# Next weights split ahead of the value loops, two tiles for the value copies, and TensorE in program order with its transposes two units late

## The chip, the cores and the metric

One core of a Trainium2 chip runs the kernel. The metric is the device time of one execution in microseconds (us). PE is the matrix engine (TensorE), DVE the vector engine, ACT the scalar engine, POOL GpSimd, SP the engine whose queue issues the DMAs here.

## The reference

The kernel computes one block of a streaming encoder over 1024 tokens of width 1024, in float32: three token mixers in parallel (multi-head latent attention, MLA; forgetting attention, FoX; a state-space mixer), a gated merge, and a gated MLP. What the change touches is the end of MLA's projections, the projection `u = hn @ w_in` for FoX and for the gate `z`, and FoX's normalisation and decay sums:

```python
hn = rms_norm(x, norm_mix_g[l])
u = hn @ w_in[l]
u_mla, u_fox, u_ssm, u_gate = jnp.split(u, split_at, axis=-1)
# fox_branch
q, k, v, f_raw = jnp.split(u, [FOX_WIDTH, 2 * FOX_WIDTH, 3 * FOX_WIDTH], axis=-1)
q = rms_norm(q.reshape(Bsz, S, FOX_HEADS, FOX_HEAD_DIM), q_gain)
k = rms_norm(k.reshape(Bsz, S, FOX_HEADS, FOX_HEAD_DIM), k_gain)
v = v.reshape(Bsz, S, FOX_HEADS, FOX_HEAD_DIM)
log_f = jax.nn.log_sigmoid(f_raw.astype(jnp.float32) + b_f.astype(jnp.float32))
F = jnp.transpose(jnp.cumsum(log_f, axis=1), (0, 2, 1))
# ssm_branch
z, xBC, dt_raw = jnp.split(u, [SSM_INNER, SSM_INNER + SSM_XBC], axis=-1)
```

## The kernel before, in words

Every float32 operand of a product is split into a high and a low part (`split`, lines 138 to 143: ACT writes the high part, line 142, DVE the rest, line 143), and `mm3` (line 167) sums three products for each of 8 blocks of the inner dimension: 24 matmuls a unit. Tokens come in 8 tiles of 128.

From about 95 to 426 us these things run:

- The MLA loop (`for t in range(NT)`, lines 450 to 507): for each token tile the products q and kv, a normalisation (`rq`), a rotation on POOL (`rope`, lines 443 to 448, of which the last instruction, line 448, writes `qn`), four groups of transposes (tiles `tp`, line 500), copies of those out of PSUM (`sh` by ACT, line 503; `sl` by DVE, line 504), and stores to DRAM (`q_h`, `q_l`, `k_h`, `k_l`, line 507). `sh` and `sl` have two buffers each; a store must land before its tile is written again.
- The value loop (lines 510 to 519): FoX's value projection, two halves of 256 columns, each of 8 tiles, each 24 matmuls (`fxv`). The products are copied and split into one tile, `fv`, with one buffer, and stored to `fv_d`. The weights are `v`, the second half's are loaded between the halves.
- 32 units of 24 matmuls with 512 columns (`fx`, lines 640 to 684): 8 of the first half of z (z0), 8 of FoX q, 8 of FoX k, 8 of the second half of z (z1); I number them 0 to 31. `load512` loads and splits their weights: four raw pieces of 512 KB each, split into `w5h` and `w5l`, each of which has two tags in turn. Raw tiles (`raw`, two buffers) come from the pool `fill`. A z unit ends in a tanh (`th`, line 654), a product (`zt`, line 656) and a store. A FoX unit ends in a square on ACT (`fsq`, line 661), a sum (`fss`, line 663), 12 small DVE operations of an inverse root (`rsqrt`, lines 148 to 159, on `rs_i`, `rs_t`, `rs_v`, `fr`) behind one on `fv` (line 665), the normalised tile (`fqn`, line 669), a group of four transposes on PE (line 673), copies (`fsh` on ACT, `fsl` on DVE) and stores.
- `gate_sums` (lines 560 to 612): cumulative sums and transposes (lines 562 to 609) for the decays.
- `down_sums` (lines 627 to 638), at two of every five units up to the 27th: two loads of 512 KB (`ws`), four sums on POOL (lines 633 to 636), two stores (`wsum_d`), work for the MLP at the end.

Behind these come the weights `wr`, `wh`, `wl` of the next projection (lines 741 to 745) and MLA's attention (lines 794 and 884).

No queue's order is written by hand here: a scheduler with a model of the engines lays the instructions of each engine in one fixed list, and each engine works through its list in order, waiting on semaphores. The loads and stores of this stretch are all issued by SP. Tiles are taken from pools that are stacked on the left or the right side of SBUF; a pool that opens where a closed one lay has its first writes wait for the last users of the old tiles. Before, `cos`, `sin`, the MLA loop's inputs (pool `chp`), its weights (`upp`) and its working tiles (`mp`) close together with the value loop's pool `fvp`, and `fill` and the units' pool `xp` open behind them.

## Time and profile before

| what | value |
|---|---|
| median of three runs | 2149.49 us (2144.91 to 2150.79) |
| the profiled execution's own time | 2144.91 us |
| its span in the trace | 2143.0 us |
| PE busy | 2042.3 us, 95% of the span |
| DVE, ACT, POOL busy | 1402.9, 936.0, 649.0 us |
| mean granted clock of PE | 0.982 |

The profiled execution was the fastest of the three; 1.9 us of it lie around the span. Rows of a timeline give the start in us, the duration in us, the engine, line and operation, what is written and read, and in brackets how long the engine stood idle before it and what ended that. A row of waits gives the engine, what it wanted to start, what it waited for, the sum, the count and the longest. The granted clock is 1.00 at 2.4 GHz and 0.50 at 1.2 GHz.

### The profile page before, as it was taken

To read this page: it belongs to the slowest core of one execution; us is meant where nothing else is said; L and a number is where in the kernel's file an instruction comes from. 1 tells how busy PE (TensorE), PEld (TensorE's weight loads), DVE (VectorE), ACT (ScalarE), POOL (GpSimd) and SP (SyncE) were. 2 spreads that over 40 slices of the span, in tenths; PEclk is the share of its full clock that TensorE was granted. 3 is DMA by queue.
4 is the path that set the end of the run, shared out by engine and by line. 5 is a ranking of instruction groups with operands and counts; after the bars stand their busy time and mean duration, and the time that the engine had idled before them with its cause. 6 is when DMAs were issued, how large, how long until landed. Compare 5 with 4: busy or idle time off the path is not lost.

```text
span 2143.0 us, 29100 instructions
## 1 busy us (share of the span) xinstructions
PE 2042.3 (95%) x10253; PEld 1689.7 (79%) x10253; DVE 1402.9 (65%) x2590; ACT 936.0 (44%) x1677; POOL 649.0 (30%) x620
## 2 busy tenths in 40 slices
PE   7999898999999999999999799999889999999999
PEld 6898677778888787787777688888668888887887
DVE  6687477346666566665888446557976677665665
ACT  5554222145555555554555213223444454545432
POOL 2453132212222222220000021002655544441855
PEclk9999999999999999999999899999899999999999
DMA  5167668654343544524342556441122222229765
GB/s 169 33 190 222 220 216 240 205 156 126 96 137 97 138 121 109 131 86 127 105 134 89 162 184 204 140 134 61 49 86 82 88 79 80 88 74 338 260 217 190
DMA packets 276649, 303.61 MB, mean 142 GB/s; under 512 B 19308, under 2 KB 209784, under 8 KB 276504
## 3 DMA queue, kind: packets, MB, share of 16 engines
q1 hardware_dynamic: 276504, 301.76, 46.0%
q8 instruction: 81, 1.33, 0.3%
q14 instruction: 64, 0.52, 0.1%
HBM read 209.03 MB, written 92.67 MB: 141 GB/s over the span
## 4 chain that ended last, share of the span: by engine, by line
PE 78%; DVE 7%; DMA 5%; POOL 3%; ACT 3%; issue 3%; SPq 0%; DVEq 0%; ACTq 0%; POOLq 0%
PE mm L794 16%; PE dn L1626 10%; PE ybr L167 8%; PE ua L1319 5%; PE fx L167 5%; PE uc L1319 5%; PE ud L1319 4%; PE wo L1364 4%; PE s L884 3%; PE tp L952 2%; PE ub L1319 2%; PE fxv L167 1%; DMA raw<-in_w_in_dram 1%; PE kv L167 1%; PE q L167 1%
## 5 line engine op out<-in xcount | busy, mean ns | idle before, releaser
L794 PE MATMUL mm<-hnh,wh 128*128 128x512 f32 x576 | 248.6, 432 | 0.0
L906 POOL TENSOR_SCALAR pm<-pm,rs 128x128 f32<-128x128 f32 (+7 forms) x128 | 110.2, 864 | 402.6 <-DVE rs L905 242.1
L794 PE MATMUL mm<-hnh,wl 128*128 128x512 f32 x576 | 226.9, 394 | 0.0
L794 PE MATMUL mm<-hnl,wh 128*128 128x512 f32 x576 | 226.1, 393 | 0.0
L1626 PE MATMUL dn<-dr,dr 128*128 128x512 f32 x592 | 182.1, 389 | 0.0
L899 ACT ACTIVATE pm<-s,nmx 128x128 f32<-128x128 f32 (+2 forms) x192 | 110.2, 579 | 97.6 <-DVE nmx L896 70.2
L958 DVE TENSOR_TENSOR ptl<-tp,pth 128x512 fp32r<-128x512 f32 (+1 forms) x160 | 100.2, 633 | 70.3 <-ACT pth L957 68.7
L889 DVE TENSOR_REDUCE nmx<-s 128x1 f32<-128x128 f32 (+2 forms) x192 | 105.5, 553 | 56.6 <-PE s L887 44.6
L884 PE MATMUL s<-qk,qk 96*128 96x384 f32 (+5 forms) x480 | 120.8, 356 | 13.0 <-ACT pm L899 11.4
L957 ACT ACTIVATE pth<-tp 128x512 fp32r<-128x512 f32 (+1 forms) x160 | 88.1, 554 | 99.5 <-PE tp L952 99.0
L1626 PEld LDWEIGHTS dn<-dr,dr 128*128 128x128 f32 x592 | 111.1, 188 | 22.9
L794 PEld LDWEIGHTS mm<-hnh,wl 128*128 128x128 f32 x576 | 108.4, 188 | 25.1
L794 PEld LDWEIGHTS mm<-hnl,wh 128*128 128x128 f32 x576 | 109.2, 190 | 17.1 <-issue 2.9
L794 PEld LDWEIGHTS mm<-hnh,wh 128*128 128x128 f32 x576 | 109.5, 190 | 16.6 <-issue 2.9
L1235 POOL TENSOR_TENSOR mg<-mg,gl 128x512 f32<-128x512 f32 x16 | 24.9, 1561 | 311.4 <-DVE gl L1232 311.3
L1626 PE MATMUL dn<-dr 128*128 128x512 f32 x296 | 115.2, 389 | 0.0
L167 PE MATMUL fx<-w5h,hnh 128*128 128x512 f32 x256 | 101.9, 402 | 7.9 <-ACT w5h L142 7.9
L143 DVE TENSOR_TENSOR dr<-dr,dr 128x1024 fp32r<-128x1024 f32 x52 | 75.3, 1449 | 49.9 <-ACT dr L142 41.8
L142 ACT ACTIVATE wh<-wr 128x1024 fp32r<-128x1024 f32 (+1 forms) x46 | 42.0, 913 | 147.6 <-PE ybr L167 69.6
L884 PEld LDWEIGHTS s<-qk,qk 96*128 96x128 f32 (+1 forms) x480 | 81.3, 192 | 26.4 <-ACT pm L899 16.2
L167 PE MATMUL ybr<-ah,wh 128*128 128x512 f32 x256 | 100.2, 396 | 1.6 <-ACT ah L142 1.6
L167 PE MATMUL fx<-w5h,hnl 128*128 128x512 f32 x256 | 101.4, 397 | 0.0
(457 smaller groups left out, 5855.7 us busy)
## 6 DMA issues: line engine op xcount, KB each, us to landing
dr<-act_d SPq DMA_DIRECT2D x99, 256.0 KB
wr<-in_ffn_w_up_dram SPq DMA_DIRECT2D x47, 512.0 KB
wr<-in_w_in_dram SPq DMA_DIRECT2D x36, 512.0 KB
g_d<-t SPq DMA_DIRECT2D x24, 512.0 KB
gl<-g_d SPq DMA_DIRECT2D x24, 512.0 KB
ws<-in_ffn_w_down_dram SPq DMA_DIRECT2D x22, 512.0 KB
wsum_d<-ws SPq DMA_DIRECT2D x22, 512.0 KB
act_d<-fa SPq DMA_DIRECT2D x22, 512.0 KB
```

What stands on the lines that cost most here:

```text
L143: return i, le.tensor_sub(l, src, f32(h))
L167: T.matmul(ps, a(k), b(k), start=(i == 0), stop=(i == n - 1))
L794: T.matmul(ps, a[:, k, :], b[half][:, k, :], start=(k == 0 and i == 0), stop=(k == NK - 1 and i == 2))
L884: T.matmul(ps[:, :w], q_[:, qs], k_[:, a:a + w], start=i_ == 0, stop=not last and i_ == len(o.passes) - 1)
L889: later(c + 0.1, lambda ps=ps, ci=ci, a=a, b=b: V.reduce_max(nmx[:, ci:ci + 1], ps[:, :b - a], axis=AX, negate=True))
L899: pss[ci][1][0] = later(c + 0.9 + 0.1 * ci, lambda ci=ci, a=a, b=b: A.activation(p_[:, a:b], pss[ci][0][:, :b - a], AF.Exp, bias=nb, accum ...
L906: G.tensor_scalar(p_[:, 0:n * P], p_[:, 0:n * P], rs[:, 3:4], 0.0, op0=ALU.mult, op1=ALU.add)
L957: later(c + 0.05, lambda th=th, pt=pt, off=off: A.activation(th[:, :off], pt[:, :off], AF.Copy))
L958: pl[0] = later(c + 0.6, lambda th=th, tl=tl, pt=pt, off=off: V.tensor_sub(tl[:, :off], pt[:, :off], f32(th[:, :off])))
L1319: T.matmul(ps, a, b, start=first and n == 0, stop=n == 11, skip_group_check=not first)
L1364: T.matmul(p, a, b, start=k == 0 and i == 0, stop=k == NK - 1 and i == 2)
L1626: T.matmul(ps[m], a[:, ts_], b[:, 512:], start=first_ and j == 0 and q == 0, stop=j == NFH - 1 and q == 2, skip_group_check=not first_)
```

## The change

- The pools `fvp` and `upp` go to a stack of their own on the right side (`pup`). The MLA loop's pools close right behind that loop, and `xp` opens in their place, ahead of the value loop.
- The second half's value weights (`v2`) and the first z weights (`w_z0`) are loaded and split ahead of both halves of the value loop in the program text; `v2` takes the tile tagged `w5l1`, and all four raw pieces of the z weights lie in the tile tagged `w5h1` (`w5r`), so that they need no raw buffers.
- The value products' copies of the second half take two tiles in turn (tags `fsh`, `fsl`) instead of the one `fv`.
- The units are built with PE's list in program order (`manual_schedule`), and the transposes of a FoX unit are called when two more units have been called (`waiting`, `turned`). `gate_sums` is a generator, of which one part is called after each unit from the first FoX unit on.

```diff
-    pmla = ExitStack()
+    pmla, pup = ExitStack(), ExitStack()
...
-        upp = pmla.enter_context(TP("upp", 1, side="right"))
+        upp = pup.enter_context(TP("upp", 1, side="right"))
...
-        fvp = pm.enter_context(TP("fvp", 1))
+        fvp = pup.enter_context(TP("fvp", 1, side="right"))
...
-        for c0 in (0, 256):
+    pmla.close()
+    px = ExitStack()
+    xp = px.enter_context(TP("xp", 2))
+    fpl = None
+    units = 0
+
+    def load512(c0):
+        n = units // NT % 2
+        h = xp.tile([P, NK, 512], F32R, name=uid("w5h"), tag=f"w5h{n}", bufs=1)
+        l = xp.tile([P, NK, 512], F32R, name=uid("w5l"), tag=f"w5l{n}", bufs=1)
+        if fpl is None:
+            raws_ = f32(xp.tile([P, NK, 512], F32R, name=uid("w5r"), tag="w5h1", bufs=1))
+        for k in range(0, NK, 2):
+            raw = raws_[:, k:k + 2, :] if fpl is None else fpl.tile([P, 2, 512], F32, name=uid("raw"), tag="wr")
+            SY.dma_start(raw, w_inv[:, k:k + 2, c0:c0 + 512])
+            split(h[:, k:k + 2, :], l[:, k:k + 2, :], raw)
+        return h, l
+
+    v2 = xp.tile([P, NK, 2, 256], F32R, name="v2", tag="w5l1", bufs=1)
+    for k in range(0, NK, 2):
+        raw = fvp.tile([P, 2, 256], F32, name=uid("raw"), tag="vr", bufs=2)
+        SY.dma_start(raw, w_inv[:, k:k + 2, C_FQ + 1280:C_FQ + 1536])
+        split(v2[:, k:k + 2, 0, :], v2[:, k:k + 2, 1, :], raw)
+    vcols.append((v2[:, :, 0, :], v2[:, :, 1, :]))
+    w_z0 = load512(C_Z)
+    for c0 in (0, 256):
+        vh, vl = vcols[c0 // 256]
+        for t in range(NT):
+            p = acc("fxv", "mv")[:, 0:256]
+            mm3(p, tok(hnh, t), tok(hnl, t), lambda k: vh[:, k, :], lambda k: vl[:, k, :], NK)
             if c0:
-                vcols.append(load_cols(fvp, "v", C_FQ + 1024 + c0, 256, 1))
-            vh, vl = vcols[-1]
-            for t in range(NT):
-                p = acc("fxv", "mv")[:, 0:256]
-                mm3(p, tok(hnh, t), tok(hnl, t), lambda k: vh[:, k, :], lambda k: vl[:, k, :], NK)
+                vt = xp.tile([P, 4, P], F32R, name=uid("fv"), tag=("fsh", "fsl")[t % 2], bufs=1)
+            else:
                 vt = fvp.tile([P, 4, P], F32R, name=uid("fv"), tag="fv", bufs=1)
-                split(vt[:, :, 0:64], vt[:, :, 64:128], p.rearrange("p (h d) -> p h d", d=64))
-                SY.dma_start(fv_d[t * P:(t + 1) * P, c0 // 64:c0 // 64 + 4, :], f32(vt))
-    pmla.close()
+            split(vt[:, :, 0:64], vt[:, :, 64:128], p.rearrange("p (h d) -> p h d", d=64))
+            SY.dma_start(fv_d[t * P:(t + 1) * P, c0 // 64:c0 // 64 + 4, :], f32(vt))
+    pup.close()
...
         T.matmul(pc[:, 64:128], ones, lf.rearrange("p t h -> p (t h)"), start=True, stop=True)
+        Ab = bcast(ssm_A_log[0], 16, "Ab", fp)
...
+        yield
...
+        trim = ft("trim", (P, P))
+        V.tensor_copy(trim, tri)
+        V.tensor_scalar_add(trim[0:64, :], trim[0:64, :], -1.0)
+        yield
...
         cum = ft("cum", (P, P))
         V.tensor_copy(cum, pd[:, 384:512])
+        yield
+        yield
         pt = tps([P, P])
         T.transpose(pt, cum, ident)
...
-    with ExitStack() as px:
-        xp = px.enter_context(TP("xp", 2))
...
+    with px:
...
-        units = 0
-        for which in (3, 0, 1, 4):
-            if which == 0:
-                gate_sums()
-            c0 = (C_FQ, C_FQ + 512, C_FQ + 1024, C_Z, C_Z + 512)[which]
-            wh, wl = load512(c0)
-            for t in range(NT):
-                if units % 5 in (1, 3) and units // 5 * 2 + units % 5 // 2 < NFH:
-                    down_sums(units // 5 * 2 + units % 5 // 2)
-                p = acc("fx", "mv" if units % 3 == 2 else "mm")
-                units += 1
-                mm3(p, tok(hnh, t), tok(hnl, t), lambda k: wh[:, k, :], lambda k: wl[:, k, :], NK)
...
-                    pt = tps()
-                    for j in range(4):
-                        T.transpose(pt[:, j, :], qn[:, 2 * j:2 * j + 2, :].rearrange("p h d -> p (h d)"), ident)
...
+        gs = gate_sums()
+        waiting = []
+
+        def turned(which, t, qn):
+            pt = tps()
+            for j in range(4):
+                T.transpose(pt[:, j, :], qn[:, 2 * j:2 * j + 2, :].rearrange("p h d -> p (h d)"), ident)
+            col = (fq_col, fk_col)[which]
+            sh = xp.tile([P, 4, P], F32R, name=uid("fsh"), tag="fsh", bufs=1)
+            sl = xp.tile([P, 4, P], F32R, name=uid("fsl"), tag="fsl", bufs=1)
+            A.activation(sh, pt, AF.Copy, scale=col)
+            V.scalar_tensor_tensor(out=sl, in0=pt, scalar=col, in1=f32(sh),
+                                   op0=ALU.mult, op1=ALU.subtract)
+            for dst, st in zip(((fq_h, fq_l), (fk_h, fk_l))[which], (sh, sl)):
+                dv_ = dst.rearrange("(a b) d s -> b d a s", b=2)
+                for b in range(2):
+                    SY.dma_start(dv_[b, 0:64, :, t * P:(t + 1) * P], f32(st[64 * b:64 * b + 64, :, :]))
+
+        with tc.manual_schedule(engines={mybir.EngineType.PE}):
+            for which in (3, 0, 1, 4):
+                c0 = (C_FQ, C_FQ + 512, C_FQ + 1024, C_Z, C_Z + 512)[which]
+                wh, wl = load512(c0) if units else w_z0
+                for t in range(NT):
+                    if units % 5 in (1, 3) and units // 5 * 2 + units % 5 // 2 < NFH:
+                        down_sums(units // 5 * 2 + units % 5 // 2)
+                    p = acc("fx", "mv" if units % 3 == 2 else "mm")
+                    units += 1
+                    mm3(p, tok(hnh, t), tok(hnl, t), lambda k: wh[:, k, :], lambda k: wl[:, k, :], NK)
+                    if which != 3:
+                        next(gs, None)
+                    if waiting and waiting[0][0] <= units - 2:
+                        turned(*waiting.pop(0)[1:])
...
+                        qn = xp.tile([P, 8, 64], F32, name=uid("fqn"), tag="fqn")
+                        V.tensor_mul(qn, p.rearrange("p (h d) -> p h d", d=64),
+                                     r.unsqueeze(2).to_broadcast([P, 8, 64]))
+                        waiting.append((units, which, t, qn))
```

PE's list at the end of the MLA loop (`tp` with `qn` or `kn` are the loop's transposes, `fxv` value products, `v_2971` and `v_2744` the second half's value weights). Before:

```order
L167 MATMUL fxv_3018<-v_2971,hnh_128 128x256
L167 MATMUL fxv_3018<-v_2972,hnh_128 128x256
L167 MATMUL fxv_3018<-v_2971,hnl_130 128x256
L500 MATMUL tp_2548<-ident,qn_2445 96x128 x4
L500 MATMUL tp_2559<-ident,qn_2445 96x128 x4
L167 MATMUL fxv_2989<-v_2971,hnh_128 128x256
```


and now:

```order
L500 MATMUL tp_2581<-ident,kn_2519 96x128 x4
L500 MATMUL tp_2695<-ident,qn_2592 96x128 x4
L500 MATMUL tp_2706<-ident,qn_2592 96x128 x4
L500 MATMUL tp_2717<-ident,kn_2666 96x128 x4
L500 MATMUL tp_2728<-ident,kn_2666 96x128 x4
L167 MATMUL fxv_3008<-v_2744,hnh_128 128x256
L167 MATMUL fxv_3037<-v_2744,hnh_128 128x256
```


The second half's value products stood between the transposes of the last two token tiles; now all these transposes come first, and the first of the products stands behind them.

SP's list at the same place (`k_h`, `k_l` are the last stores of the MLA loop, `raw_3272` and `w5r_2763` the first z weights, `raw_2753` and `raw_2757` the second half of the value weights, `fv` the value products' stores). Before:

```order
L507 DMA k_h<-sh_2733 96x4x128
L507 DMA k_l<-sl_2723 96x4x128
L507 DMA k_l<-sl_2734 96x4x128
L519 DMA fv_d<-fv_3130 128x512
L532 DMA b_3235<-in_fox_b_f_dram 128x8
L533 DMA b_3235<-in_ssm_dt_bias_dram 128x16
L623 DMA raw_3272<-in_w_in_dram 128x2x512
L623 DMA raw_3276<-in_w_in_dram 128x2x512
```


and now:

```order
L507 DMA k_l<-sl_2723 96x4x128
L507 DMA k_h<-sh_2733 96x4x128
L507 DMA k_l<-sl_2734 96x4x128
L524 DMA w5r_2763<-in_w_in_dram 128x2x512 x4
L531 DMA raw_2753<-in_w_in_dram 128x2x256
L531 DMA raw_2757<-in_w_in_dram 128x2x256
L558 DMA b_3252<-in_fox_b_f_dram 128x8
```


The four pieces of the z weights stand directly behind the loop's stores, ahead of the last two pieces of the value weights.

PE's list at the transposes of unit 16, the first of FoX k (`fqn_4274` before, `fqn_4259` now; `fx_4429` is unit 19 of before, `fx_4337` unit 18 and `fx_4401` unit 19 of now). Before:

```order
L167 MATMUL fx_4429<-w5h_4195,hnl_130 128x512
L673 MATMUL tp_4276<-ident,fqn_4274 128x128 x4
L167 MATMUL fx_4429<-w5h_4195,hnh_128 128x512
L167 MATMUL fx_4429<-w5l_4196,hnh_128 128x512
L167 MATMUL fx_4429<-w5h_4195,hnl_130 128x512
```


and now:

```order
L167 MATMUL fx_4337<-w5l_4168,hnh_128 128x512
L167 MATMUL fx_4337<-w5h_4167,hnl_130 128x512
L665 MATMUL tp_4362<-ident,fqn_4259 128x128 x4
L167 MATMUL fx_4401<-w5h_4167,hnh_128 128x512
L167 MATMUL fx_4401<-w5l_4168,hnh_128 128x512
```


The group stood three matmuls into unit 19; now it stands at the end of unit 18.

DVE's list there (`fr_871` and `fr_863` belong to unit 16, `fqn_4180` to unit 15; `raw_4783` is the third raw piece of the z1 weights of before, `raw_4759` the fourth of now). Before:

```order
L669 TENSOR_TENSOR fqn_4180<-fx_4131,fr_847_4162 128x512
L149 TENSOR_SCALAR fr_871_4256<-rs_i_4257 128x8
L157 TENSOR_TENSOR rs_t_4262<-fr_871_4256 128x8
L143 TENSOR_TENSOR w5l_4774<-raw_4783,w5h_4773 128x1024
L158 TENSOR_TENSOR rs_t_4262<-rs_t_4262,rs_v_4260 128x8
```


and now:

```order
L704 TENSOR_SCALAR fv_876_4303<-fss_4301 128x8
L159 SCALAR_TENSOR_TENSOR fr_863_4241<-rs_t_4255,fr_863_4241 128x8
L143 TENSOR_TENSOR w5l_4746<-raw_4759,w5h_4745 128x1024
L148 TENSOR_SCALAR rs_i_4306<-fv_876_4303 128x8
L151 TENSOR_SCALAR rs_v_4309<-fv_876_4303 128x8
L708 TENSOR_TENSOR fqn_4259<-fx_4197,fr_863_4241 128x512
```


Before, the split of the third piece stood inside unit 16's chain; now the fourth piece's stands there, right ahead of its last steps, and the third's stands ahead of unit 15's `fqn`.

## Rows read from the trace of the kernel before

**Rows 1.** the page, part 4: the chain that ended last, share by engine

```profile
PE 78%; DVE 7%; DMA 5%; POOL 3%; ACT 3%; issue 3%; SPq 0%; DVEq 0%; ACTq 0%; POOLq 0%
```

**Rows 2.** waits of PE in 95 to 440 us: total, times, longest

```profile
PE fx L167 <- ACT w5h L142: 7.9, 1, 7.9
PE tp L673 <- DVE fv L665: 6.1, 1, 6.1
PE fxv L167 <- DVE fv L143: 3.3, 3, 2.3
PE tp L673 <- DVE fqn L669: 2.3, 1, 2.3
PE tp L609 <- DVE Fl L143: 1.4, 1, 1.4
```

**Rows 3.** busy us by stretch: PE, PEld, DVE, ACT, POOL; granted clock; DMA share; GB/s

```profile
340.00:350.00 10.00, 3.87 (x14) 3.01 (x13) 9.62 (x22) 4.47 (x7) 3.76 (x3) 0.65 0.77 236
350.00:360.00 10.00, 10.00 (x41) 8.02 (x40) 7.54 (x28) 2.24 (x3) 0.00 (x0) 0.84 0.84 231
```

**Rows 4.** timeline of ACT: start, duration, instruction, idle before and its releaser

```profile
272.46 0.60 ACT L654 ACTIVATE th<-fx 128x512 f32<-128x512 f32 x1 [4.85 <-PE fx L167]
305.30 0.60 ACT L661 ACTIVATE fsq<-fx 128x512 f32<-128x512 f32 x1 [0.94 <-PE fx L167]
311.22 0.60 ACT L661 ACTIVATE fsq<-fx 128x512 f32<-128x512 f32 x1 [0.93 <-PE fx L167]
...
404.78 0.60 ACT L654 ACTIVATE th<-fx 128x512 f32<-128x512 f32 x1 [4.84 <-PE fx L167]
```

**Rows 5.** timelines of POOL, SP, DVE, ACT at the loop's end

```profile
199.39 0.45 POOL L448 TENSOR_TENSOR qn<-rp,rp 128x128 f32<-128x128 f32 x1
...
206.56 1.04 SPq L507 DMA_DIRECT2D q_l<-sl  x2
210.29 1.38 SPq L507 DMA_DIRECT2D k_l<-sl  x2
213.78 1.07 SPq L623 DMA_DIRECT2D raw<-in_w_in_dram  x2
228.65 6.40 SPq L623 DMA_DIRECT2D raw<-in_w_in_dram  x3
...
209.51 0.75 DVE L504 SCALAR_TENSOR_TENSOR sl<-tp,gk_col,sh 96x512 fp32r<-96x512 f32 x1 [1.65 <-DMA q_l<-sl]
...
232.34 1.06 ACT L142 ACTIVATE w5h<-raw 128x1024 fp32r<-128x1024 f32 x1 [4.35 <-DMA raw<-in_w_in_dram]
234.34 1.06 ACT L142 ACTIVATE w5h<-raw 128x1024 fp32r<-128x1024 f32 x1 [0.94 <-DMA raw<-in_w_in_dram]
```

**Rows 6.** timelines of SP, ACT, DVE, POOL around the longest wait

```profile
332.21 0.43 SPq L623 DMA_DIRECT2D raw<-in_w_in_dram  x1
...
338.95 1.06 ACT L142 ACTIVATE w5h<-raw 128x1024 fp32r<-128x1024 f32 x1 [8.25 <-DMA raw<-in_w_in_dram]
...
340.04 1.23 DVE L143 TENSOR_TENSOR w5l<-raw,w5h 128x1024 fp32r<-128x1024 f32 x1 [4.27 <-ACT w5h L142]
341.58 1.19 DVE L157 TENSOR_TENSOR rs_t<-fr 128x8 f32<-128x8 f32 x1
...
341.49 1.26 POOL L634 TENSOR_TENSOR ws<-ws,ws 128x512 f32<-128x512 f32 x1 [3.98 <-DMA ws<-in_ffn_w_down_dram]
```

**Rows 7.** timeline of DVE in the units

```profile
302.40 0.68 DVE L663 TENSOR_REDUCE fss<-fsq 128x8 f32<-128x512 f32 x1
303.73 0.17 DVE L157 TENSOR_TENSOR rs_t<-fr 128x8 f32<-128x8 f32 x1
306.81 0.67 DVE L663 TENSOR_REDUCE fss<-fsq 128x8 f32<-128x512 f32 x1
313.59 1.28 DVE L159 SCALAR_TENSOR_TENSOR fr<-rs_t,fr 128x8 f32<-128x8 f32 x1
...
389.01 1.13 DVE L159 SCALAR_TENSOR_TENSOR fr<-rs_t,fr 128x8 f32<-128x8 f32 x1
```

More of the change, by code (lines that the diff above doesn't have):

```diff
@@ L600, in gate_sums @@
         V.tensor_mul(dend, dend, dt)
-        trim = ft("trim", (P, P))
-        V.tensor_copy(trim, tri)
-        V.tensor_scalar_add(trim[0:64, :], trim[0:64, :], -1.0)
         T.matmul(pd[:, 384:512], trim, dv, start=True, stop=True)
@@ L612, in gate_sums @@
         SY.dma_start(cum_d.rearrange("a r s -> r a s"), f32(ct))
-    with ExitStack() as px:
-        xp = px.enter_context(TP("xp", 2))
-        def load512(c0):
-            h = xp.tile([P, NK, 512], F32R, name=uid("w5h"), tag=f"w5h{units // NT % 2}", bufs=1)
-            l = xp.tile([P, NK, 512], F32R, name=uid("w5l"), tag=f"w5l{units // NT % 2}", bufs=1)
-            for k in range(0, NK, 2):
-                raw = fpl.tile([P, 2, 512], F32, name=uid("raw"), tag="wr")
-                SY.dma_start(raw, w_inv[:, k:k + 2, c0:c0 + 512])
-                split(h[:, k:k + 2, :], l[:, k:k + 2, :], raw)
-            return h, l
+    with px:
         def down_sums(k):
@@ new lines, in block_kernel @@
+        with tc.manual_schedule(engines={mybir.EngineType.PE}):
[12 more added lines that the diff above has]
+                        turned(*waiting.pop(0)[1:])
+                    if which > 2:
+                        th = xp.tile([P, 512], F32, name=uid("th"), tag="fsq")
+                        A.activation(th, p, AF.Tanh, scale=0.5)
+                        zt = xp.tile([P, 512], F32, name=uid("zt"), tag="fqn")
+                        V.scalar_tensor_tensor(out=zt, in0=th, scalar=1.0, in1=p, op0=ALU.add, op1=ALU.mult)
+                        zc = 512 * (which - 3)
+                        SY.dma_start(z_d[t * P:(t + 1) * P, zc:zc + 512], zt)
+                    else:
+                        sq = xp.tile([P, 512], F32, name=uid("fsq"), tag="fsq")
+                        A.activation(sq, p, AF.Square)
+                        ss = xp.tile([P, 8], F32, name=uid("fss"), tag="fss")
+                        V.reduce_sum(ss, sq.rearrange("p (h d) -> p h d", d=64), axis=AX)
+                        v = xp.tile([P, 8], F32, name=uid("fv8"), tag="fv8")
+                        V.tensor_scalar(v, ss, 1.0 / 64, EPS, op0=ALU.mult, op1=ALU.add)
+                        r = xp.tile([P, 8], F32, name=uid("fr8"), tag="fr8")
+                        rsqrt(xp, r, v, 8)
+                        qn = xp.tile([P, 8, 64], F32, name=uid("fqn"), tag="fqn")
+                        V.tensor_mul(qn, p.rearrange("p (h d) -> p h d", d=64),
+                                     r.unsqueeze(2).to_broadcast([P, 8, 64]))
+                        waiting.append((units, which, t, qn))
```

40 lines of the change are left out of this document (5 added, 35 removed).

## The prediction

> **What bounds the kernel now.** I read the chain of work that ended last first: TensorE (PE) holds 78% of it [rows 1], so only what moves PE's own queue can move the end. All that the change touches lies between 180 and 426 us, and behind the last unit of that stretch both programs issue the same instructions in the same order, so I take a shift of that end as a shift of the kernel's end, one for one. Next I read what PE waited for in 95 to 440 us [rows 2]: 7.9 us once for the first z weights, 3.3 us for the single value tile and, in the forgetting-attention (FoX) units, 1.4, 6.1 and 2.3 us. The granted clock by stretch [rows 3] adds what a wait leaves behind: after the 6.1 us wait PE ran at the lower of its two levels for some 6 us.
>
> A unit of 24 matmuls takes 0.60 + 4.84 = 5.44 us without transposes, 311.22 - 305.30 = 5.92 us with them [rows 4]; so one 512-column matmul is 0.227 us, and a 256-column one of the value loop I take at half, 0.114 us (an estimate from that row). PE finished the last z0 unit of before at about 272.3 us [rows 4]. The working goes in two halves: until z0 ends, and from there to the end of the units.
>
> **Until z0 ends: later.** The change wants the next weights split ahead of the value loops, but v2, w5h0 and w5l0 take SBUF that the MLA loop's tiles held. Their first writes wait for the end of that loop, and the 192 matmuls of the value projection's second half, which before filled PE from 184 to 219 us, now stand behind the last MLA transposes. So PE has nearly nothing from 184 us until those weights are there.
>
> When are they there? SP issues the four 512 KB pieces straight behind the last k_l store of tile 7. Before, tile 7's rotation on POOL ended at 199.39 + 0.45 = 199.8 us, and the last k_l store went out by 210.29 + 1.38 = 211.7 us [rows 5]. In that tail PE placed value units between the transposes; without them I add up the dependent steps: 1.0 us for eight q transposes (four lengthen a unit by 0.48 us), 1.3 for two copies (taken as long as the subtraction's 0.75 or a little less), 0.75 for the first subtraction, 2.9 until a q store frees its tile (q_l went out from 206.56 us and the subtraction that waited for it started at 209.51) and 1.5 for two more subtractions: 7.4 us behind the rotation, 207.2 us. ACT and DVE also lose the value tiles' copies in that stretch, which can bring the rotation itself forward by up to 3 us; I take 205.5 us. The bounds are 203 (rotation 4 us earlier) and 211.7 us (nothing in the tail gets shorter); I stand near the early end because the waits that shorten are PE's own.
>
> From issue to ACT's split the first piece took 232.34 - 228.65 = 3.7 us and the next 2.0 us more [rows 5]; four pieces take 3.7 + 3 x 2.0 = 9.7, and the last split 1.06 + 1.23 = 2.3 us [rows 5, 6]. So the last piece is ready at 205.5 + 9.7 + 2.3 = 217.5 us. By PE's new order 19 z matmuls and 26 value matmuls can go ahead of it; 173 and 166 are left: 173 x 0.227 + 166 x 0.114 = 39.2 + 18.9 = 58.1 us, that is 275.6 us. After 20 idle us PE comes back at the lower level; the 6.1 us wait cost (1 - 0.65) x 3.87 + (1 - 0.84) x 10 = 3.0 us of clock [rows 3], and here part of it falls on the sparse start, so I add 2.4 us. Z0 ends at 278.0 us instead of 272.3: **+6 us**, from +2 (early issue, no clock loss) to +13 (issue at 211.7). The two tiles for the value copies remove a wait of 3.3 us [rows 2], which lies inside this sum already. What is late next there is the store queue: on SP the stores that free the two tiles stand behind down-sum stores that wait for POOL. By my sum of the steps the third value unit's copy finds its tile free with about a microsecond to spare; I take nothing, and up to +3 us in the range.
>
> **From z0 to the end of the units: earlier.** Between 272.3 and the last unit PE lost 1.4 + 6.1 + 2.3 = 9.8 us of waiting [rows 2] and the 3.0 us of clock, 12.9 with rounding. How much goes? Program order on PE puts each transpose group behind unit u+2. The list before already ran two units late or more: the group that waited 6.1 us, that of unit 16, stood 3 matmuls into unit 19, which is even 0.7 us later than the new place. So the new place alone does not remove that wait; it goes only if unit 16's normalised tile is ready sooner. Why was it late? The raw piece of the z1 weights was issued at 332.21 us behind a down-sum store that waited for POOL, ACT stood 8.25 us for it, DVE 4.27 us in the middle of unit 16's chain [rows 6]. In the new order the third piece's DVE split stands ahead of unit 15's last step and the fourth ahead of unit 16's, so the same hazard is there with other timing. Counting from the end of unit 12 with 5.92 us a unit: the fifth down-sum's loads go out after its q stores (+2.5 us), land 3.7 + 2.0 = 5.7 later, POOL's four operations take 4 x 1.26 = 5.0 [rows 5, 6], the q stores behind them about 2.5 (a pair took 1.04 to 1.38), with 0.8 for the next load ahead of it, so the third piece goes out at +16.5 and is split by +22.5 to +25.5; unit 15's tile is wanted at +29.5. The fourth goes out behind the next down-sum at about +26.5 and is split at +32 to +35; unit 16's tile is wanted at +35.4. It just fits, or lacks 1 us; unit 17's, with two more weight splits ahead of it, lacks 1 to 2 us. The 1.4 us wait goes: the gate sums' transposes now stand two units behind their sums. Of the 2.3 us one, of unit 23, 7 matmuls or 1.6 us go by the place. I leave 2.9 us of new waits, so this half gives **-10 us**, from -12.9 (none left) to -2 (the chain on DVE as late as before).
>
> The other edits carry no price: no matmul is added or dropped, the gate operations that move by a unit or two are wanted only by the attention stages, and ACT and DVE do as many splits as before.
>
> The sum is -10 + 6 = -4 us. The profiled execution took 2144.9 us, the fastest of the three shown; on it the sum gives 2140.9. The median is 4.6 us higher; a median of the changed kernel may lie as much above, and I add a third of that: **2142.5 us**.
>
> **The rivals.** (a) *DVE becomes the bound of the FoX units.* PE now waits strictly for the tile of two units ago. One unit costs DVE 306.81 - 302.40 = 4.41 us [rows 7] against PE's 5.92, but weight splits of 1.23 us and slow small operations come on top: while POOL runs its sums, DVE's multiply of two SBUF tiles takes 1.19 us [rows 6] instead of 0.17 [rows 7]. Fifteen instructions between 313.59 and 389.01 us were stretched so, the first and last of them in [rows 7], by about 1.0 us each: some 15 us in all. If its idle time stays as it was, fqn of unit 23 comes as late as before and only some 3 us of the 12.9 are won: -3 + 6 = +3, 2148 us on the profiled execution. For it: in the ten microseconds behind 340 us DVE was busy for 9.62 [rows 3]. Against: much of its idle time was the wait for the raw piece.
>
> The Trainium skill, "SBUF — State Buffer", section "Who interferes with whom", has a rule that speaks against this change: a VectorE instruction with two SBUF inputs and a GpSimd instruction that reads SBUF exclude one another for a whole instruction. The 1.19 us beside a POOL operation of 1.26 us [rows 6] agrees. By it all 24 POOL operations of the stretch could each hold one DVE instruction, 24 x 1.0 = 24 us instead of 15, which would bring this rival about.
>
> (b) *Slower: the first weights come no sooner than in before.* Before, the first z pieces were issued at 213.78 us [rows 5]. If tile 7's tail still waits on stores, the four pieces go out then, the last is ready at 225.8, z0 ends at 286 with the clock loss: +14. With -10 that is +4, 2149 us; from an issue at 216 us on, or when this meets rival (a), it is slower by over 6.4 us: 2144.9 + 14 - 3 = 2156. For it: 20 us in which PE has no filler at all are new, and nothing else can use them. Against: the value units that lengthened the tail are gone from it.
>
> (c) *The tail costs nothing.* If the rotation of tile 7 comes 4 us sooner and the sparse work hides the clock loss, z0 ends at +1 and all 12.9 us go: 2133 us. The change then does what its words say.
>
> **How the numbers follow.** What a measurement of this kernel tells from no change is about 0.3%, 6.4 us. My forecast (-9 to +1 us) has 0.47, nearly a third of it beyond -6.4; (a) 0.20, nearly all within; (b) 0.17, mostly beyond +6.4; (c) 0.16, all faster. That makes faster 0.32, within 0.3% 0.49, slower 0.19. The range leaves out about 0.1 on each side: from 2132, (c) with all of the gain, to 2156, (b) together with (a).
>
> **What would show it.** In the changed profile: the issue of the first z piece (205.5, at most 211.7 us); PE idle from about 184 to 205 us and the lower clock behind it; the last z0 unit at 278 us; the wait ahead of the transposes in the units, in all below 5 us; ACT's wait for the third raw piece of z1 short or harmless. The forecast is wrong if the first z piece comes after 212 us or before 203, if PE's waits between z0 and the end of the units stay above 8 us, or if the end of the units does not carry to the end of the kernel.

## The result and the profile after

The changed kernel takes 2152.28 us (median of 13 runs, 2147.12 to 2157.51), the kernel before 2147.65 us (13 runs beside them, 2143.28 to 2150.79). The ratio is 1.0027, with a 95% interval of 1.0016 to 1.0038: slower by 0.27%, or 5.8 us (the ratio goes by the means; the two medians lie 4.6 us apart). The forecast was 2142.5 us, a gain.

Executions of one program lie up to 10 us apart here, so both kernels were traced twice. Three points of the traces divide the execution: ACT's reading of the last z0 product, its reading of the last product of the units (both as in [rows 4]), and the end of the span.

| us | before | before, again | after | after, again |
|---|---|---|---|---|
| last z0 product | 272.5 | 273.4 | 280.5 | 281.8 |
| last product of the units | 426.5 | 424.5 | 430.2 | 435.2 |
| between the two | 154.1 | 151.1 | 149.7 | 153.4 |
| from there to the end of the span | 1716.5 | 1715.2 | 1720.0 | 1719.7 |
| span | 2143.0 | 2139.7 | 2150.2 | 2154.9 |

On the means of the two: **z0 ends 8.2 us later, the units take 1.0 us less, and what follows takes 4.0 us more**. The forecast had +6, -10 and 0. (The means of the two pairs of traces lie 11 us apart, the medians 4.6; so the three terms show where the time goes, and are generous in size. Two traces of one kernel differ by more than the middle one.)

The waits of PE in 95 to 440 us, which answer [rows 2] (engine, line waited for: total, times, longest):

```profile
PE tp L665 <- DVE fqn L708: 4.2, 2, 3.6
PE tp L500 <- POOL qn L448: 4.0, 1, 4.0
PE tp L500 <- DVE rs_t L157: 3.7, 1, 3.7
PE tp L500 <- DVE sl L504: 3.3, 2, 2.6
...
PE fxv L167 <- ACT v L142: 2.8, 1, 2.8
PE fx L167 <- ACT w5h L142: 1.5, 1, 1.5
PE fxv L167 <- DVE fv L143: 1.1, 1, 1.1
```

The 7.9 us for the first z weights became 1.5, and the single value tile's 3.3 became 1.1. In their place stand 4.0 + 3.7 + 3.3 + 2.8 = 13.8 us in the tail of the MLA loop (L500 is the loop's transposes); in before no wait of those transposes reached 0.7 us. In the units 4.2 us for `fqn` are left of 6.1 + 2.3, with three shorter waits of 0.6 to 1.0 us further down the list.

The tail by stretches of ten microseconds from 180 us (columns as in [rows 3]):

```profile
180.00:190.00 10.00, 5.95 (x42) 4.98 (x40) 7.99 (x24) 5.79 (x11) 3.98 (x9) 0.81 0.89 264
190.00:200.00 10.00, 3.57 (x16) 2.83 (x16) 4.45 (x7) 2.63 (x5) 5.67 (x8) 0.50 0.68 177
200.00:210.00 10.00, 6.44 (x28) 5.17 (x27) 4.19 (x6) 3.27 (x6) 0.00 (x0) 0.50 0.80 210
210.00:220.00 10.00, 7.72 (x31) 6.03 (x31) 6.50 (x9) 5.27 (x6) 0.00 (x0) 0.83 0.89 316
```

PE is busy for 23.7 of the 40 us; in before it was for 34.0, with a granted clock of 1.00, 0.98, 0.85 and 1.00. In after it holds 0.50, its lower level of 1.2 GHz, for the 20 us in the middle. PE's timeline there, the last four groups of eight transposes (start, duration, instruction, idle before and its releaser):

```profile
187.94 1.91 PE L500 MATMUL tp<-ident,qn 128*96 128x128 f32 x8 [3.75 <-DVE rs_t L157]
192.41 1.95 PE L500 MATMUL tp<-ident,kn 128*96 128x128 f32 x8 [2.56 <-DVE sl L504]
198.38 1.94 PE L500 MATMUL tp<-ident,qn 128*96 128x128 f32 x8 [4.02 <-POOL qn L448]
201.02 1.94 PE L500 MATMUL tp<-ident,kn 128*96 128x128 f32 x8 [0.70 <-DVE sl L504]
```

Between one group and the next stands nothing; in before the second half's value products stood there (57 matmuls of both kinds in 190 to 200 us, now the 16 of the transposes). SP's and ACT's timelines show what waits for the tail's end (start, duration, what is issued or done):

```profile
205.99 0.30 SPq L507 DMA_DIRECT2D k_l<-sl  x1
206.40 2.23 SPq L524 DMA_DIRECT2D w5r<-in_w_in_dram  x4
...
211.37 1.06 ACT L142 ACTIVATE w5h<-w5r 128x1024 fp32r<-128x1024 f32 x1 [5.15 <-DMA w5r<-in_w_in_dram]
...
215.45 1.06 ACT L142 ACTIVATE w5h<-w5r 128x1024 fp32r<-128x1024 f32 x1 [0.30 <-DMA w5r<-in_w_in_dram]
...
280.47 0.60 ACT L693 ACTIVATE th<-fx 128x512 f32<-128x512 f32 x1 [4.84 <-PE fx L167]
...
430.16 0.60 ACT L693 ACTIVATE th<-fx 128x512 f32<-128x512 f32 x1 [4.84 <-PE fx L167]
```

The first z weights go out at 206.40 us instead of 213.78 [rows 5], 7.4 us sooner, and z0 still ends 8.0 us later.

In the units the longest wait left is unit 17's. POOL's, SP's, ACT's and DVE's rows ahead of it:

```profile
338.93 1.31 POOL L655 TENSOR_TENSOR ws<-ws,ws 128x512 f32<-128x512 f32 x1
...
340.67 0.57 SPq L657 DMA_DIRECT2D wsum_d<-ws  x1
341.29 0.44 SPq L524 DMA_DIRECT2D raw<-in_w_in_dram  x1
...
351.16 0.56 SPq L768 DMA_DIRECT2D wr<-in_w_in_dram  x1
...
355.27 1.06 ACT L771 ACTIVATE wh<-wr 128x1024 fp32r<-128x1024 f32 x1 [3.27 <-DMA wr<-in_w_in_dram]
...
356.36 1.22 DVE L772 TENSOR_TENSOR wl<-wr,wh 128x1024 fp32r<-128x1024 f32 x1 [1.65 <-ACT wh L771]
...
358.87 0.68 DVE L708 TENSOR_TENSOR fqn<-fx,fr 128x512 f32<-128x512 f32 x1
359.47 0.80 DVE L159 SCALAR_TENSOR_TENSOR fr<-rs_t,fr 128x8 f32<-128x8 f32 x1
```

It is the chain of [rows 6] one link further on. The fourth raw piece goes out behind the store of a down-sum that POOL ended at 340.2 us. The next weight pieces follow late, and DVE, which runs its list in order, stands 1.65 us for one of them with unit 17's last steps behind it. So the wait moved to another weight split and shrank, from 6.1 us to 3.6 (5.4 in the second trace of after), but did not go.

### The profile page after: what moved, and what is told of

The parts are those of the page before. It is cut to its first block, busy times and chain, and to the rows that moved or that the text cites. A ratio compares the mean times of both kernels' runs of the same rounds, so it can differ in the third digit from the quotient of the medians.

```text
span 2150.2 us, 29070 instructions
## 1 busy us (share of the span) xinstructions
PE 2045.9 (95%) x10238; PEld 1693.7 (79%) x10253; DVE 1405.3 (65%) x2590; ACT 935.1 (43%) x1677; POOL 650.5 (30%) x620
## 4 chain that ended last, share of the span: by engine, by line
PE 81%; DVE 7%; DMA 4%; ACT 3%; POOL 3%; issue 2%; SPq 1%; ACTq 0%; DVEq 0%; POOLq 0%
PE mm L821 16%; PE dn L1653 9%; PE ybr L167 8%; PE fx L167 5%; PE ua L1346 5%; PE uc L1346 5%; PE ud L1346 4%; PE wo L1391 4%; PE s L911 4%; PE tp L979 3%; PE ub L1346 2%; PE cq L167 2%; PE fxv L167 1%; PE ckv L167 1%; PE q L167 1%
## 5 line engine op out<-in xcount | busy, mean ns | idle before, releaser
L821 PEld LDWEIGHTS mm<-hnl,wh 128*128 128x128 f32 x576 | 109.8, 191 | 17.2 <-issue 2.9
L167 PE MATMUL fx<-w5l,hnh 128*128 128x512 f32 x256 | 101.2, 395 | 0.8 <-DVE w5l L143 0.8
```

Of the source, the lines that this page charges most:

```text
L167: T.matmul(ps, a(k), b(k), start=(i == 0), stop=(i == n - 1))
L821: T.matmul(ps, a[:, k, :], b[half][:, k, :], start=(k == 0 and i == 0), stop=(k == NK - 1 and i == 2))
```

## Experiments

Two theories stood against each other. **A**: program order with transposes two units late takes waits out of the units, and the tail costs something apart from that. **B**: the program order is worth nothing; the units end when the chain of POOL, SP and DVE lets them, so a late start looks like a gain in the units, and the whole price is in the tail, where PE lost its filler.

### One half of the change at a time

The first kernel is before with the units and `gate_sums` of after, the second is after with the units and `gate_sums` of before (its head kept).

```diff
 # e1_units: before, with
+        with tc.manual_schedule(engines={mybir.EngineType.PE}):
...
+                    if waiting and waiting[0][0] <= units - 2:
+                        turned(*waiting.pop(0)[1:])
 # e2_head: after, with
-        with tc.manual_schedule(engines={mybir.EngineType.PE}):
...
+            wh, wl = load512(c0) if units else w_z0
```

> The kernel before with only the second half of the change: units in program order on TensorE, transposes two units late, gate sums in parts; pools, value loop and first z weights as before. Theory A (the change consists of a late start, about +8 us at the end of z0, and a gain in the units, about -4 us): z0 ends at 272 us as before, the units end at 421 to 423 us instead of 426.5, the kernel is 2 to 7 us faster than before. Rival B (the program order itself costs as much as it gives, and the gain seen is only a gap that the late start moved): units end at 426 or later, kernel within 1 us of before or slower.

Measured: 2147.60 us, ratio 1.0003 (0.9988 to 1.0018). From z0's end, 276.8, to the units' end, 431.2, it took 154.5 us; before took 154.1 and 151.1. So the units went as rival B said. But z0 ended 4.3 us later than in before, where 272 us had been expected. The waits of PE there, beside the 8.0 us for the first weights:

```profile
PE tp L651 <- DVE fqn L694: 6.3, 2, 5.2
...
PE tp L651 <- DVE fr L149: 1.9, 1, 1.9
PE tp L651 <- DVE Fl L143: 1.7, 1, 1.7
```

That is 9.9 us, against 9.8 in [rows 2]. Program order changed which tile is late, not how late.

Why z0 ends later shows where its first matmuls start, in before and then in e1:

```profile
227.10 2.93 PE L167 MATMUL fx<-w5h,hnh 128*128 128x512 f32 x6 [7.93 <-ACT w5h L142]
```

```profile
227.42 0.80 PE L167 MATMUL fx<-w5h,hnh 128*128 128x512 f32 x1 [7.97 <-ACT w5h L142]
228.99 0.79 PE L167 MATMUL fx<-w5l,hnh 128*128 128x512 f32 x1 [0.78 <-DVE w5l L143]
```

The scheduler's list gave PE six matmuls on the first high part that was there; program order gave it one, and PE waited for the low part. From 220 to 240 us PE was busy for 12.9 us in before, at a granted clock of 0.83, and for 10.0 us in e1, at 0.74.

> The changed kernel with only the first half of the change: pools, second value half and first z weights ahead of the value loops, two copy tiles; the units in the scheduler's order as before. Theory A: the second value half and the z weights wait for the end of the latent-attention loop, TensorE idles and runs at the lower clock from 188 to 212 us, z0 ends at 279 to 282 us, the units end some 8 us later than before (434 to 436) and the kernel is 6 to 13 us slower. Rival B (the late start is made good by waits that it shortens in the units): units end at 427 to 430, kernel 0 to 4 us slower.

Measured: 2148.50 us, ratio 1.0008 (0.9996 to 1.0020). ACT reads the last z0 product at 275.2 us, and the first FoX product 6.7 us behind it, as in before (272.5 and 279.2 us there):

```profile
275.21 0.60 ACT L668 ACTIVATE th<-fx 128x512 f32<-128x512 f32 x1 [4.85 <-PE fx L167]
...
281.95 0.60 ACT L675 ACTIVATE fsq<-fx 128x512 f32<-128x512 f32 x1 [3.75 <-PE fx L167]
```

The units end at 429.6 us and take 154.4 us, as long as in before and e1, with 9.1 us of waits ahead of transposes:

```profile
PE tp L687 <- DVE fqn L683: 6.1, 4, 2.6
...
PE tp L635 <- DVE Fl L143: 2.4, 1, 2.4
```

The kernel is as late as rival B said, but not for its reason: the head alone starts the units only 2.7 us late, not 8, and shortens nothing in them. Against e2, program order (after) ends z0 5.3 us later in the first trace and 6.6 in the second, and takes 4.7 and 1.0 us out of the units; its units end no sooner (430.2 and 435.2 us). The two halves alone read 0.6 and 1.7 us slower, together 5.8; the intervals do not say whether they add up.

### The filler put back

E3 is after with the loading of the second half's value weights inside the value loop again. There PE has the second half's products for the tail, as in before. The last four copies still use the two tiles.

```diff
-    v2 = xp.tile([P, NK, 2, 256], F32R, name="v2", tag="w5l1", bufs=1)
...
+        if c0:
+            vcols.append(load_cols(fvp, "v", C_FQ + 1024 + c0, 256, 1))
+        vh, vl = vcols[-1]
...
-            if c0:
+            if c0 and t > 3:
```

> The changed kernel with the second value half's weights back in the value loop's own tiles, loaded between the halves as before (and the first four of its copies in the single tile), so that TensorE has the value products beside the last transposes; first z weights still ahead, units in program order. Theory A (it is the missing filler that makes the change late, not the early z weights): no idle time of TensorE over 3 us between 184 and 215 us, z0 ends at 264 to 268 us instead of 272 (before) and 280 (changed), the kernel is 8 to 14 us faster than before. Rival C (the z weights are what comes late, whatever fills the time): z0 ends at 272 us or later, the kernel is no more than 5 us faster.

Measured: 2140.20 us, ratio 0.9966 (0.9951 to 0.9980), faster than before by 7.3 us and than after by some 13. The two middle stretches, which answer after's:

```profile
190.00:200.00 10.00, 8.32 (x64) 7.31 (x64) 8.34 (x24) 4.38 (x7) 2.54 (x2) 1.00 0.92 266
200.00:210.00 10.00, 8.87 (x76) 8.69 (x75) 3.59 (x8) 3.58 (x8) 2.54 (x6) 1.00 0.72 204
```

and SP's issue of the first z weights, in the timeline:

```profile
211.88 2.32 SPq L524 DMA_DIRECT2D w5r<-in_w_in_dram  x4
```

The weights go out 5.5 us later than in after, and z0 still ends 15.6 us earlier, at 264.9 us: PE is busy for 17.2 instead of 10.0 us in these two stretches, at full clock instead of half. When the weights come is worth little here; what PE does until then is worth much. The kernel as a whole gained a little less than theory A said (8 to 14 us). But the units take 158.8 us here: of 15.6 us won at z0, 6.5 are left at their end (423.7).

E9 has e3's head and the scheduler's units:

> The head of e3 (value products beside the last transposes, z weights ahead) with the units in the scheduler's order as before, so without the program order. If the program order with two units' delay is worth nothing by itself (as e1 against before, and e2 against the changed kernel, show), z0 ends at 263 to 267 us, the units at 422 to 426 and the kernel is like e3: 0.2 to 0.5% faster than before. If it is worth 4 us, this kernel is 3 to 5 us slower than e3 (2143 to 2146 us).

Measured: 2139.02 us, ratio 0.9964 (0.9950 to 0.9978), z0 at 260.0, units' end at 418.1: 158.1 us. Both points come earlier than expected, the time as expected. All six kernels together, by head and by the order of the units (end of z0, end of the units: between the two; us):

| head | scheduler's order | program order, two units late |
|---|---|---|
| of before | before: 272.5, 426.5: 154.1; again 273.4, 424.5: 151.1 | e1: 276.8, 431.2: 154.5 |
| of after | e2: 275.2, 429.6: 154.4 | after: 280.5, 430.2: 149.7; again 281.8, 435.2: 153.4 |
| with the filler | e9: 260.0, 418.1: 158.1 | e3: 264.9, 423.7: 158.8 |

In every row program order ends z0 later, by 3 to 7 us, more than the 0.9 and 1.3 us by which two traces of one kernel differ there, and in no row does it end the units sooner. In part its first z pieces go out later (206.40 us in after against 204.36 in e2, 211.88 in e3 against 208.60 in e9), in part PE has less to do while they come, as in e1. The medians do not resolve these few microseconds (0.9966 against 0.9964 with the filler). Theory A is out, for a delay of two units; B is right on the units, but the tail is not the whole price of the change: of after's 8.0 us at z0, e2's head has 2.7. In each column the filler takes some 15 us off the end of z0. Units that start at 260 to 265 us take 158 to 159 us, later ones 150 to 155; that a late start shortens them fits this table, and no run shows it apart from the head.

### What holds the units

Two kernels are before with changed down-sums. E7 leaves out the seven that lie in the FoX units (their results are missing, and seven stores of other data of the same size go out later); its time as a whole says nothing. E10 leaves out POOL's operations of those seven alone: loads and stores stay, and the raw weights are stored in place of the sums.

```diff
 # e7_no_sums_before
-                if units % 5 in (1, 3) and units // 5 * 2 + units % 5 // 2 < NFH:
+                if which > 1 and units % 5 in (1, 3) and units // 5 * 2 + units % 5 // 2 < NFH:
 # e10_no_pool_before
-            G.tensor_sub(s12[:, 0, :], w1[:, 1, :], w1[:, 0, :])
...
+            if k not in range(3, 10):
+                G.tensor_sub(s12[:, 0, :], w1[:, 1, :], w1[:, 0, :])
...
+            else:
+                s12, s34 = w1, w2
```

> The kernel before without the seven down-sums that fall into the FoX units: their loads and POOL operations are left out, and their place in DRAM is filled with other numbers at the end of the last unit (7 MB of stores come there, so only the time up to the units' end is read). If POOL's operations beside DVE and the stores that wait for POOL ahead of the weight pieces on SP make the units' waits: no 6.1 us wait, DVE's small operations at 0.17 us, and the stretch from z0's end to the units' end takes 140 to 146 us instead of 154.1. If they do not: 151 us or more.

> The kernel before with the loads and stores of the seven down-sums in the FoX units, but without their POOL operations (the loaded weights are stored as they are). Between before (154.1 us from z0's end to the units' end; 151.1 in its second trace) and e7 (140.9 us, no down-sums): if POOL beside DVE, and stores that wait for POOL ahead of the weight pieces, make the waits, the stretch comes to 141 to 145 us; if the 14 MB of transfers make them, to 149 us or more.

Measured: the units take 140.9 us in e7, without a wait on PE, and 142.5 us in e10, with this one, both as expected:

```profile
PE tp L676 <- DVE fqn L672: 1.4, 1, 1.4
```

So the 14 MB that these sums move are nearly free (1.6 us between these two traces), and POOL's operations cost before 9 to 12 us. They can do so in two ways, by the stores that wait for them on SP with weight pieces behind, and by DVE's slowness beside them; e10 takes both away at once, so their shares are not shown. Counting DVE's 128x8 operations between 282 and 432 us that took over 0.4 us instead of 0.17: 16 and 17 in the two traces of before (15.8 and 16.7 us beyond 0.17 each), 20 and 24 in those of after (19.9 and 24.2 us), none in e10. The Trainium skill, "SBUF — State Buffer", section "Who interferes with whom", which the prediction weighed, agrees in kind: without POOL no stretched operation is left. 2 of the 16 in before read one tile only (`fr` from `rs_i` at 328.06 us took 1.26 us), which the rule, as the prediction tells it, does not cover. The prediction's bound by that rule, 24 operations, was reached in one trace of after (these seven sums have 28 POOL operations).

E11 takes the same seven sums out of after, in the manner of e7:

> The changed kernel without the seven down-sums of the FoX units (left out as in e7, 7 MB of stores behind the last unit; read up to the units' end). With the down-sums gone, program order has nothing left to gain over the scheduler's order: stretch from z0's end 139 to 142 us (149.7 with them; e7 took 140.9), units' end at 419 to 423 us. If program order itself costs waits: 145 us or more.

Measured: 281.4 to 429.8, 148.4 us. That is the second case of the expectation, 145 us or more. One wait of 3.9 us is left, for unit 16's tile, beside one of 0.7. SP's, ACT's, DVE's and PE's rows there:

```profile
340.84 0.56 SPq L771 DMA_DIRECT2D wr<-in_w_in_dram  x1
...
346.11 1.06 ACT L774 ACTIVATE wh<-wr 128x1024 fp32r<-128x1024 f32 x1 [3.07 <-DMA wr<-in_w_in_dram]
...
347.20 1.23 DVE L775 TENSOR_TENSOR wl<-wr,wh 128x1024 fp32r<-128x1024 f32 x1 [1.67 <-ACT wh L774]
...
349.74 1.23 DVE L775 TENSOR_TENSOR wl<-wr,wh 128x1024 fp32r<-128x1024 f32 x1 [0.29 <-ACT wh L774]
...
351.37 0.69 DVE L711 TENSOR_TENSOR fqn<-fx,fr 128x512 f32<-128x512 f32 x1
...
352.20 1.09 PE L665 MATMUL tp<-ident,fqn 128*128 128x128 f32 x4 [3.90 <-DVE rs_t L157]
```

and the stretch with the wait:

```profile
345.00:360.00 15.00, 11.10 (x39) 8.80 (x38) 9.91 (x41) 3.87 (x5) 0.00 (x0) 0.77 0.72 180
```

Even without POOL's sums two splits of the next projection's weights stand in DVE's list ahead of the last step of unit 16's chain (`fqn` at 351.37), and DVE stands 1.67 us for the first of them to land. The stretch has the wait (15 - 11.1 us) and the clock behind it, by estimate (1 - 0.77) x 15 = 3.5 us. So 3.9 + 3.5 = 7.4 us, and 148.4 - 7.4 = 141.0, close to e7's 140.9. In the changed kernel the weight splits' place on DVE is a cause of its own; whether it comes with the order or with the head, this run does not tell.

### Three units late

E5 is after with the transposes one unit later still, and a third `fqn` tile for it, which `zt` shares (`mn` shares `rec`'s tile, to make room). E6 is e3 with the same edit. The later place and the third tile were not tried apart.

```diff
-                    if waiting and waiting[0][0] <= units - 2:
+                    if waiting and waiting[0][0] <= units - 3:
...
-                        qn = xp.tile([P, 8, 64], F32, name=uid("fqn"), tag="fqn")
+                        qn = xp.tile([P, 8, 64], F32, name=uid("fqn"), tag="fqn", bufs=3)
```

> The changed kernel with the transposes three units late instead of two (a third tile for the normalised values, one gate tile shared to make room). If the units of the changed kernel lose time because two units are too short a delay for DVE's bursts, the waits ahead of the transposes fall from 5.8 us to below 1.5, the stretch from z0's end to the units' end from 149.7 to 142 to 146 us, and the kernel is 3 to 7 us faster than the changed one (2145 to 2149 us). If DVE, the weight pieces or the stores set the pace (rival a of the prediction), the waits move a unit on, the stretch stays at 148 to 151 us and the time at 2150 to 2154.

Measured: 2148.73 us, ratio 1.0008 (0.9995 to 1.0020), z0 at 280.7, units' end at 423.5: 142.8 us, as expected of a delay that was too short, and not of DVE as the bound. The transposes' waits in the units are all but gone, and the first scores of attention wait a little longer than in after (1.1 and 0.9 us there):

```profile
PE s L912 <- issue: 1.8, 1, 1.8
PE s L912 <- DMA qk<-q_l: 1.1, 1, 1.1
...
PE tp L666 <- DVE fsl L671: 0.5, 1, 0.5
PE tp L666 <- DVE fqn L709: 0.4, 1, 0.4
```

The units' end came 3.1 us before that of before in its first trace, but the span ended 4.7 us after it. So 7.8 us went behind the units, 3.0 of them by 475 us, in the start of attention.

> The kernel of e3 (value products beside the last transposes) with the transposes three units late. There z0 ended at 264.9 us and the stretch to the units' end took 158.8 us: longer than in any other kernel here. If the delay of two units is what is too short, the stretch falls to 143 to 150 us and the units end at 408 to 415, the kernel at 2126 to 2133 us. If something else (DVE's work, the order of the weight pieces behind the down-sum stores) fixes the units' end nearly in absolute time, the stretch stays at 155 us or more and the kernel at 2138 to 2142.

Measured: **2134.31 us, ratio 0.9947 (0.9928 to 0.9965): 11 us faster than before and some 17 faster than after, the best kernel here.** Z0 at 263.1, units' end at 411.7 (148.6 us), span 2129.4. The units' end and their stretch came as expected, the time 1 us above. The filler brings 0.0061 of the ratio with either delay. The third unit brings 0.0019 with either head, which the intervals alone do not show; the traces do, with 148.6 us in the units against e3's 158.8. Two waits of 2.7 us each are left there.

### Does a later end of the units carry to the end?

E4 is before with 16 matmuls more (3.6 us, by 0.227 us each) ahead of the last unit. Its product is rewritten by the unit's own first matmul.

```diff
+                if units == 32:
+                    for i in range(16):
+                        T.matmul(p, tok(hnh, t)(0), wh[:, 0, :], start=(i == 0), stop=(i == 15))
```

> The kernel before with 16 more matmuls of 512 columns ahead of the last z1 unit (their sum is overwritten): 3.6 us more of TensorE at the end of the units and nothing else. If a shift of the units' end carries to the kernel's end one for one: +3.6 us. If, as between the two profiled executions, a shift of 3.6 us there grows to 7 us by clock that is granted lower behind short waits of the attention stages: +5.5 to +8 us, with granted clock below 0.95 in stretches at 440, 590 or 725 us where before shows 1.00.

Measured: 2150.33 us, ratio 1.0014 (0.9997 to 1.0030), so +3.0 us of 3.6 (-0.6 to +6.4). In its trace the units' end is 5.4 us late and the span 10.0. The medians speak for a carry near one for one, the single trace for a loss behind it; that is inconclusive. Two kernels were therefore traced a second time:

> The kernel before, unchanged, for a second trace of it. If a trace's differences behind the units' end are differences between executions: the units end within 1 us of 426.5, and the shift against the first trace changes by 1 us or more at some of the places where the traces of the changed kernel and of the others jump (590, 725, 1220, 1560 us), with granted clock below 1.00 at one trace and not the other. If they belong to the kernel: shift below 0.5 us throughout.

> The changed kernel, unchanged, for a second trace. If the growth of the shift behind the units' end (from 3.6 to 7.1 us in the first pair of traces) is a difference between executions: the steps at 590, 725, 1220 and 1560 us are other ones here, the units end at 428 to 432 us and the end of the kernel differs from the first trace by 2 us or more. If it belongs to the kernel: the same steps at the same places.

Measured: 2141.62 and 2156.97 us (spans in the table). The units ended 2.0 us earlier and 5.0 us later than in the first traces, both outside what was expected. Against the first trace of before, both traces of after lose 1.5 us at some 590 us and 1.0 us at some 725 us, and no trace of before does. Stretches around the first place, before and then after (columns as in [rows 3]):

```profile
580.00:590.00 10.00, 8.08 (x45) 6.39 (x43) 9.86 (x20) 4.45 (x13) 2.55 (x2) 1.00 0.20 52
590.00:600.00 10.00, 10.00 (x59) 8.32 (x59) 6.27 (x19) 6.03 (x18) 2.91 (x3) 1.00 0.68 205
```

```profile
580.00:590.00 10.00, 9.26 (x55) 7.78 (x53) 7.30 (x14) 3.74 (x7) 2.43 (x2) 1.00 0.23 59
590.00:600.00 10.00, 8.82 (x40) 7.20 (x41) 7.38 (x20) 6.40 (x18) 2.02 (x3) 0.83 0.26 91
```

Both have the same wait of 1.9 us for ACT's `pm`; before keeps the clock through it, after loses it for some microseconds behind it. That explains 2.5 of the 4.0 us behind the units. Why the same wait costs the clock in one and not in the other is left open, and the other kernels of this series show both steps, one or none. In e1 and e2, whose units also end late, what follows takes 1712.8 and 1713.0 us, less than in before.

## Why the prediction was wrong

**Until z0 ends (+6; measured +8.0 and +8.4): right.** SP issued the first z piece at 206.40 us (said: 205.5, bounds 203 to 211.7), because the memory of the MLA loop holds the weights back, and PE had nearly nothing in between. The landing was too dear: four pieces issued back to back were split 1.35 us apart, not 2.0, so the last was ready at about 217.7 us, as forecast in spite of the later issue (215.45 + 1.06 on ACT, and DVE's split of 1.2). What the sum had too low lies behind that piece. PE had then done 12 z and 24 value matmuls, not 19 and 26, after 20 us at a clock of 0.50; the 2.4 us added for the clock cover about that. From there it needed 62.8 us at a clock of 1.00, not 58.1: beside the 9 matmuls more (1.8 us), three value matmuls took 0.36 us, not 0.34, and the wait of 1.1 us for a copy's tile had been taken at nothing. E3 shows that the missing filler makes z0 late: the same early z weights with the filler left in end z0 at 264.9 us. What the prediction did not see is that the head is not alone: with the scheduler's order it ends z0 at 275.2 us (e2), and program order brings the rest.

**From z0 to the units' end (-10; measured -4.4 and +2.3, -1.0 on the means): this is the step that failed.** The prediction saw that the list of before already ran two units late, that a new place alone removes no wait, and that the wait goes only if the normalised tile is ready sooner. It then summed up a chain that "just fits, or lacks 1 us" and left 2.9 us of new waits. In after's first trace 6.5 us of waits and 1.7 us of clock are left, 8.2 of the 12.9; in the second 9.9 us of waits, as many as in before. The mis-sized term is the chain on DVE: unit 17's tile, said to lack 1 to 2 us, lacked 3.6 and 5.4, and unit 16's, which was to fit or lack 1 us, lacked 1.0 and 1.1. The prediction counted the two weight splits ahead of unit 17's and gave no working for when they land; DVE stood 1.65 us for one of them in after, and 1.67 us for one in e11 even without POOL's sums. E1, e2 and e9 show the step's error directly: the two-unit program order never ends the units sooner, with any of the three heads. What the units take less in after than in e2 (4.7 and 1.0 us) z0 takes more (5.3 and 6.6).

**Rival (a), DVE as the bound of the units, came nearest in size and not in mechanism.** It said that some 3 of the 12.9 us would be won and gave 2148; 1.0 us was won on the means. It had a chance of 0.20, against 0.47 for a chain that fitted by one microsecond. DVE's chain is what comes late, and the row that spoke for it, DVE busy for 9.62 of 10 us from 340 us on [rows 3], and the fifteen stretched operations should have weighed more; the argument against it, that much of DVE's idle time was the wait for one raw piece, failed since the next piece was late in its place. But DVE is no bound: in e5 it does the same work and the units take 142.8 us. Its work comes in bursts for which two units are too short a delay.

**Rival (b)** had the sign and not the mechanism: the first weights came 7 us sooner than before. **Rival (c)** did not occur.

**"A shift of that end is a shift of the kernel's end, one for one": not borne out by the traces.** Behind the units' end after takes 4.0 us more; 2.5 of them are two clock losses at 590 and 725 us. E4's medians are compatible with one for one, e5's hardly (-3.1 us at the units' end in its trace, -1.1 to +4.3 on the whole). How much of a gain or loss is kept there in general is open.

In all: 8.2 - 1.0 + 4.0 = +11.2 us on the traces, against +6 - 10 = -4. Of the 15 us between, 9 are the units' term, 4 the carry, 2 the tail.

## What to carry to other kernels

Before moving a load forward at the cost of the work that covers its wait, price the cover: here 7 us earlier weights lost against the missing filler and the clock behind it, and the two together, with the filler left in, won 13 us over the change. Putting one engine's list in program order gains nothing where its waits come from another engine's chain, and costs where the list had let the engine go ahead with other products while weights come; give the chain more time (here one unit more, with a third tile) or shorten it. When a sum says that a chain "just fits", the forecast should be that it does not. And a gain between two marks should be read together with where the first mark lies: here most of what left the units had gone to z0.

## What the runs showed of the hardware

- A VectorE operation on 128x8 elements took 0.17 us alone and mostly 1.1 to 1.3 us beside a POOL operation of 1.3 us; without POOL's operations none of some 16 was stretched, with the same DMA traffic.
- Four 512 KB pieces issued back to back reached ACT 5.0 us after the first issue and then 1.35 us apart.
- A wait of 1.9 us in attention left the granted clock at 1.00 in both traces of before, and at 0.83 and 0.87 over ten microseconds at it or behind it in those of after.
